# SwiGLU by seven products: 1024-column operations and two running sums in PSUM

## The chip, the cores and the metric

The kernel runs on one core of a Trainium2 chip. The metric is the device time of one execution in microseconds (us); a kernel's time is the median of its runs. The kernel computes in fp32 throughout, with every large matrix product split into three products of parts (see below).

## The reference

The model is a two-layer decoder on 512 tokens of width 1024. Each layer is half a SwiGLU, a mixer, and half a SwiGLU again, so there are four SwiGLUs, called ffn0 to ffn3 here. The change touches three of them; the mixers (`mlstm_mixer`, `nsa_shared_kv`, `nsa_mixer`) are left out.

```python
D_MODEL, SEQ, DEPTH, D_FF = 1024, 512, 2, 2816

def rmsnorm(x, g):
    xf = x.astype(jnp.float32)
    y = xf * lax.rsqrt(jnp.mean(xf * xf, axis=-1, keepdims=True) + EPS)
    return (y * g.astype(jnp.float32)).astype(x.dtype)

def swiglu(h, w_in, w_out):
    a, b = jnp.split(h @ w_in, 2, axis=-1)
    return (jax.nn.silu(a) * b) @ w_out

def reference(x, ...):
    h = x
    for layer in range(DEPTH):
        h = h + 0.5 * swiglu(rmsnorm(h, ffn_norm[layer, 0]), ffn_w_in[layer, 0], ffn_w_out[layer, 0])
        hn = rmsnorm(h, mix_norm[layer])
        ...
        h = h + 0.5 * swiglu(rmsnorm(h, ffn_norm[layer, 1]), ffn_w_in[layer, 1], ffn_w_out[layer, 1])
        ...
    return h
```

## The kernel before

Everything is held transposed: features lie on the 128 partitions and the 512 tokens along the columns, so the stream `h` is 8 tiles of 128 x 512. The stages run in the order ffn0, mlstm, ffn1, kv, ffn2, nsa, ffn3. The kernel is written in a tile language: a scheduler orders each engine's instructions ahead of time by its own estimate of durations, and each engine then runs its list strictly in that order, waiting on semaphores.

**Parts.** TensorE (PE) multiplies in a rounded fp32 format. So each operand is split (`split`, L232) into `hi`, its rounded value, made by ScalarE (ACT, L233), and `lo`, the rest, made by VectorE (DVE, L234). `mm3` (L226) then issues three matmuls into the same sum: hi by hi, hi by lo, lo by hi. Weights are split while they are loaded: `load_weight` (L135; L161 on ACT, L162 on DVE) for whole strips of 1024 columns, `load_forms` (L193) for the sums of quarters described next.

**Order of the weights.** A dry run first records in which order the weights are asked for (`plan`, `weight`). In the real run `weight` loads ahead in that order until `1 + self.ahead` are ready; `ahead` is 3 in the stages in question, and there are 4 buffers each for `whi` and `wlo`. So a split for the fourth weight from now waits until PE has finished with the oldest.

**One SwiGLU** (`ffn`, L364) has 22 blocks of 128 for the gate `a` and 22 for `b`, p = 0 to 21. They run in three chunks (`EVENS`: 8, 8 and 6 blocks), two blocks at a time. A pair of output blocks is computed either plainly (`strip`: 2 blocks x 8 k x 3 = 48 matmuls of 512 columns) or as a unit of seven products (`by_seven`, L447). In ffn0, ffn1 and ffn3 the blocks p = 0 and 1 (gate and `b`) and the gates of p = 2 and 3 are plain; there remain 9 gate units (`GATES`) and 10 `b` units, 19 per SwiGLU.

**A unit of seven products** halves the output rows (two blocks), the inner dimension (4 k each) and the tokens (256 each), and forms the product of these 2 x 2 matrices from seven products instead of eight: 7 x 4 k x 3 = 84 matmuls of 256 columns. The sums that it needs of the weight's quarters are made by `add_quarters` (L182, four DVE operations of 512 columns, L188 to L191), those of the tokens' quarters once per SwiGLU by `x_forms` (L411). Four DMAs of 256 KB fetch the quarters (`fetch`, L166), one unit ahead. The seven weight forms are split one at a time, 512 columns each. The products go to four PSUM banks X, Y, Z, V, and are put together by one ACT copy (L468) and five DVE operations, three of 256 columns (L473, L478, L488) and two of 512 (L476, L483).

**Gating.** `silu` (L389) multiplies the gate by the row scale `r` (L392, DVE) and takes Silu (L394, ACT), per block of 512 columns; `gate` (L397) multiplies by the `b` part (L401), in the last chunk also that part by `r` (L400, since `fold` is off there), and splits the result to `ghi`, `glo`.

**Output.** After each chunk, for each pair m of the 8 output blocks, `mm3` runs over that chunk's blocks (8, 8 or 6) into two PSUM banks; each block is then added to `h` (L589 and L590 where `fold`, L586 in the last chunk). For the pair m = 0 the order goes by k first, so that the freshest gated blocks are needed last. After the last chunk the next stage's `norm_in` (L265) reads `h`: it makes `xhi`, `xlo` and the sum of squares (L288, L300), which `rstd_columns` (L326) sums on PE.

ffn2 is computed from another stage's parts and its row of `LATER` chunks; it shares this code before the change and has a function of its own after it.

Of the kernel before, what the change touches and what calls it, by code (L numbers as in the profile page):

```python
# [30 lines left out]
SEVEN = (0, 1, 3)  # L31
# [67 lines left out]
class Net:  # L99
    def __init__(self, ctx, tc, a, order=None):  # L100
# [10 lines left out]
        self.raws, self.sums = {}, {}  # L111
# [23 lines left out]
    def load_weight(self):  # L135
# [4 lines left out]
        if name == "add":  # L140
            return self.add_quarters(*idx)
        if name == "form":
            self.ready.append(((name, idx), self.load_forms(*idx)))
            return
# [37 lines left out]
    def add_quarters(self, *at):  # L182

        q = self.raws[at]
        s = self.sums[at] = {j: self.fp.tile([P, 512], F32, name=f"s{j}", tag=f"s{j}", bufs=1) for j in (1, 2, 4)}
# [7 lines left out]
    def load_forms(self, i, p, group):  # L193

        q, s = self.raws[i, p], self.sums[i, p]
# [8 lines left out]
        return out  # L204

# [14 lines left out]
    def strip(self, w, k):  # L220
        return w[0][:, k, :], w[1][:, k, :]

    def mm(self, out, lhsT, rhs, start, stop):
        self.nc.tensor.matmul(out, lhsT, rhs, start=start, stop=stop)  # L224

    def mm3(self, out, l, r, start, stop):  # L226

        self.mm(out, l[0], r[0], start, False)
        self.mm(out, l[0], r[1], False, False)
        self.mm(out, l[1], r[0], False, stop)  # L230
# [6 lines left out]
    def setup(self):  # L237
        nc, a, c = self.nc, self.a, self.const
        self.h = [self.hp.tile([P, T], F32, name=f"h{b}") for b in range(KB)]
# [124 lines left out]
    def ffn(self, i, given=None):  # L364

        nc, tc = self.nc, self.tc
        seven, r = i in SEVEN, None
        self.qbufs = 2 if seven else 1
        self.ahead = 3 if seven else 2
        TT, STT = nc.vector.tensor_tensor, nc.vector.scalar_tensor_tensor  # L370
        N = T // 2
        with ExitStack() as ctx:
            pp = ctx.enter_context(tc.tile_pool(name=f"fps{i}", bufs=8 if seven else 6, space=PSUM, reuse_waits="tile"))
# [12 lines left out]
            x, ssq = (given, None) if given else self.norm_in(G_FFN + i * KB, True, i == 0)  # L386
            ps_mm = lambda: pp.tile([P, T], F32, name="pmm", tag="mm")

            def silu(pa):  # L389
                t = gp.tile([P, T], F32, name="ft", tag="ft", bufs=3 if seven else 2)  # L390
                if seven:
                    TT(t, pa, r, op=ALU.mult)  # L392
                    pa = t
                nc.scalar.activation(t, pa, AF.Silu)  # L394
                return t

            def gate(t, u):  # L397

                if seven and not fold:
                    TT(u, u, r, op=ALU.mult)  # L400
                TT(t, t, u, op=ALU.mult)  # L401
                bufs = 8 if seven or not k0 else 6
# [4 lines left out]

            def gate_plain(pa, pb):
                gate(silu(pa), pb)

            def x_forms(k):  # L411


                g1, g2 = (self.g[:, G_FFN + i * KB + b:G_FFN + i * KB + b + 1] for b in (k, k + 4))

                one, two = (gp.tile([P, 3 * N], F32, name="fw", tag="fw", bufs=3) for _ in range(2))
                h2, c = self.h[k + 4], [two[:, N * j:N * j + N] for j in range(3)]
                nc.scalar.activation(one[:, :T], self.h[k], AF.Copy, scale=g1)
                TT(one[:, T:], one[:, N:T], one[:, :N], op=ALU.subtract)
                STT(c[0], h2[:, N:], g2, one[:, T:], op0=ALU.mult, op1=ALU.subtract)  # L420
                STT(c[1], h2[:, N:], g2, one[:, N:T], op0=ALU.mult, op1=ALU.subtract)
                STT(c[2], h2[:, :N], g2, c[0], op0=ALU.mult, op1=ALU.subtract)
                hi = gp.tile([P, 4 * N], F32R, name="thi", tag="thi", bufs=4)
                lo = gp.tile([P, 4 * N], F32R, name="tlo", tag="tlo", bufs=4)
                self.split(one[:, T:], hi[:, :N], lo[:, :N])
                self.split(two, hi[:, N:], lo[:, N:])
                xt.append((hi, lo))
# [19 lines left out]
            def by_seven(p):  # L447
# [3 lines left out]
                W = gp.tile([P, 3, N], F32, name="fw", tag="fw", bufs=1 if i == 2 else 3)  # L451
# [42 lines left out]
            def plain(p):  # L494
                if seven and p == 1:
                    upcoming("fetch", None)
                w2 = [self.weight("ffn_in", i, p + j * FB) for j in range(2)]
                if seven and p == 1:
                    upcoming("add", None)
                ps = ps_mm(), ps_mm()  # L500
                order = [(k, j) for j in range(2) for k in range(KB)]
                if p == 0:
                    order.sort(key=lambda o: o[0] + 3.5 * o[1])
                for t, (k, j) in enumerate(order):
                    if seven and p == 1 and t == 3:
                        self.rstd_columns(ssq, ps_mm())
                    if seven and p == 1 and t >= 12:
                        x_forms(t - 12)
                    strip(ps[j], w2[j], k)
                    yield  # L510
                late.append(ps)

            xt, late = [], []


            if seven:
                units = [q for p in range(2, FB, 2) for q in ((p, FB + p) if p in GATES else (FB + p,))]
            else:
                units = [q for p in range(LATER[1][0], FB, 2) for q in (p, FB + p)][1:]
# [6 lines left out]
            for k0, k1 in EVENS if seven else LATER:  # L526
                gs, fold = [], seven and k1 < FB
# [914 lines left out]
```

## Time and profile before

| | |
|---|---|
| median of 3 runs | 1980.41 us (1978.17 to 1980.75) |
| profiled execution | 1979.33 us, its span 1976.4 us, so 2.9 us lie around the span |
| stages in question | ffn0 to 356.4 us; ffn1 from 575.5 to 930.0 us; ffn3 from 1626.4 us to the end |
| TensorE clock granted | 1.00 over the span |
| DMA | 98 GB/s in the mean |

Times in the trace count from the span's start. In a row of grouped instructions the shape stands as out<-in with partitions x elements, then the count, then busy time and the mean of one in ns, then the idle time of the engine just before them and who ended it. In the timeline a row has the start, the length and the instruction, with idle time before it in brackets. Instructions of one engine overlap in the records (an instruction starts before the row of the one before has ended), so what an instruction costs its engine is the distance between two starts. In the view of stretches each engine has its busy time in that stretch and, in brackets, how many of its instructions touch it.

### The profile page before, as it was taken

To read this page: it belongs to the slowest core of one execution; us is meant where nothing else is said; L and a number is where in the kernel's file an instruction comes from. 1 tells how busy PE (TensorE), PEld (TensorE's weight loads), DVE (VectorE), ACT (ScalarE), POOL (GpSimd) and SP (SyncE) were. 2 spreads that over 40 slices of the span, in tenths; PEclk is the share of its full clock that TensorE was granted. 3 is DMA by queue.
4 is the path that set the end of the run, shared out by engine and by line. 5 is a ranking of instruction groups with operands and counts; after the bars stand their busy time and mean duration, and the time that the engine had idled before them with its cause. 6 is when DMAs were issued, how large, how long until landed. Compare 5 with 4: busy or idle time off the path is not lost.

```text
span 1976.4 us, 31792 instructions
## 1 busy us (share of the span) xinstructions
PE 1958.3 (99%) x12042; PEld 1728.6 (87%) x12042; DVE 1611.1 (82%) x2960; ACT 1009.8 (51%) x1912; POOL 165.0 (8%) x217
## 2 busy tenths in 40 slices
PE   9999999999999999999999999999999999999999
PEld 7989999788879999898888989898777778999897
DVE  8969788757888879697687969686888888879795
ACT  6525345445655435254454535355889865435242
POOL 0000001012200000000110000001434420000000
PEclk9999999999999999999999999999999999999999
DMA  5333422323132323323443333323322132323322
GB/s 189 109 99 102 123 75 73 116 87 92 59 123 86 123 81 98 103 68 112 118 131 112 110 109 104 97 70 105 92 65 65 54 96 81 121 82 98 109 72 91
DMA packets 81816, 192.79 MB, mean 98 GB/s; under 512 B 9856, under 2 KB 10752, under 8 KB 81664
## 3 DMA queue, kind: packets, MB, share of 16 engines
q1 hardware_dynamic: 80272, 188.02, 31.2%
q8 instruction: 94, 1.54, 0.3%
q0 software_dynamic: 384, 1.05, 0.3%
q10 hardware_dynamic: 1008, 1.70, 0.2%
q14 instruction: 58, 0.48, 0.1%
HBM read 177.10 MB, written 2.10 MB: 91 GB/s over the span
## 4 chain that ended last, share of the span: by engine, by line
PE 83%; DVE 8%; ACT 4%; DMA 2%; issue 1%; SPq 0%; POOL 0%; DVEq 0%; ACTq 0%
PE pmm L224 76%; PE vps L224 2%; ACT pr L1181 1%; DVE wlo L162 1%; PE S L224 1%; PE po L224 1%; PE pt L1213 1%; PE paux L224 1%; DVE ptl L234 1%; DVE nx L1177 1%; DMA q<-in_ffn_in 1%; ACT pth L233 1%; PE pn L224 1%; DVE wlo L234 1%; ACT whi L161 0%
## 5 line engine op out<-in xcount | busy, mean ns | idle before, releaser
L224 PE MATMUL pmm<-xhi,whi 128*128 128x256 f32 (+1 forms) x1376 | 446.0, 324 | 0.9 <-ACT whi L161 0.4
L224 PE MATMUL pmm<-xhi,wlo 128*128 128x256 f32 (+1 forms) x1376 | 443.3, 322 | 0.6 <-DVE wlo L162 0.6
L224 PE MATMUL pmm<-xlo,whi 128*128 128x256 f32 (+1 forms) x1376 | 443.0, 322 | 0.5 <-DVE xlo L278 0.5
L161 ACT ACTIVATE whi<-wraw 128x512 fp32r<-128x512 f32 (+3 forms) x258 | 204.0, 810 | 313.9 <-PE pmm L224 183.2
L224 PE MATMUL pmm<-thi,wlo 128*128 128x256 f32 x1184 | 335.0, 283 | 1.0 <-DVE wlo L234 1.0
L224 PE MATMUL pmm<-tlo,whi 128*128 128x256 f32 x1184 | 335.3, 283 | 0.0
L224 PE MATMUL pmm<-thi,whi 128*128 128x256 f32 x1184 | 334.6, 283 | 0.1
L224 PEld LDWEIGHTS pmm<-xhi,wlo 128*128 128x128 f32 x1376 | 261.6, 190 | 20.5 <-DVE wlo L162 1.0
L224 PEld LDWEIGHTS pmm<-xlo,whi 128*128 128x128 f32 x1376 | 261.7, 190 | 19.1 <-DVE xlo L278 2.1
L224 PEld LDWEIGHTS pmm<-xhi,whi 128*128 128x128 f32 x1376 | 261.8, 190 | 18.8 <-issue 1.1
L162 DVE TENSOR_TENSOR wlo<-wraw,whi 128x512 fp32r<-128x512 f32 (+3 forms) x258 | 238.5, 936 | 45.1 <-ACT whi L161 42.7
L224 PE MATMUL pmm<-glo,whi 128*128 128x512 f32 x704 | 274.2, 390 | 0.1
L224 PE MATMUL pmm<-ghi,wlo 128*128 128x512 f32 x704 | 273.9, 389 | 0.0
L224 PE MATMUL pmm<-ghi,whi 128*128 128x512 f32 x704 | 272.6, 390 | 0.0
L233 ACT ACTIVATE whi<-s 128x512 fp32r<-128x512 f32 x222 | 139.5, 628 | 250.8 <-PE pmm L224 141.5
L224 PEld LDWEIGHTS pmm<-thi,wlo 128*128 128x128 f32 x1184 | 226.2, 191 | 1.2 <-DVE wlo L234 1.2
L224 PEld LDWEIGHTS pmm<-thi,whi 128*128 128x128 f32 x1184 | 226.8, 192 | 0.5 <-ACT fw L468 0.5
L224 PEld LDWEIGHTS pmm<-tlo,whi 128*128 128x128 f32 x1184 | 226.4, 191 | 0.0
L233 ACT ACTIVATE whi<-q 128x512 fp32r<-128x512 f32 x260 | 161.4, 623 | 117.8 <-PE pmm L224 103.0
L234 DVE TENSOR_TENSOR wlo<-q,whi 128x512 fp32r<-128x512 f32 x260 | 180.1, 693 | 16.2 <-ACT whi L233 16.0
L224 PEld LDWEIGHTS pmm<-glo,whi 128*128 128x128 f32 x704 | 132.2, 188 | 27.4 <-DVE glo L234 0.6
L224 PEld LDWEIGHTS pmm<-ghi,wlo 128*128 128x128 f32 x704 | 132.2, 188 | 27.4
(369 smaller groups left out, 3319.2 us busy)
## 6 DMA issues: line engine op xcount, KB each, us to landing
q<-in_ffn_in SPq DMA_DIRECT2D x260, 256.0 KB, 2.8
wraw<-in_ffn_out SPq DMA_DIRECT2D x48, 512.0 KB, 3.6
wraw<-in_ffn_out SPq DMA_DIRECT2D x48, 384.0 KB, 3.2
wraw<-in_ffn_in SPq DMA_DIRECT2D x27, 512.0 KB, 3.4
e<-in_ffn_in SPq DMA_DIRECT2D x36, 256.0 KB, 2.9
wraw<-in_m_qk SPq DMA_DIRECT2D x8, 512.0 KB, 3.3
wraw<-in_m_v SPq DMA_DIRECT2D x8, 512.0 KB, 3.3
wraw<-in_m_og SPq DMA_DIRECT2D x8, 512.0 KB, 3.3
```

What stands on the lines that cost most here:

```text
L161: nc.scalar.activation(hi[:p, c], raw[:p, c], AF.Copy)
L162: nc.vector.tensor_tensor(lo[:p, c], raw[:p, c], hi[:p, c].bitcast(F32), op=ALU.subtract)
L224: self.nc.tensor.matmul(out, lhsT, rhs, start=start, stop=stop)
L233: self.nc.scalar.activation(hi, src, AF.Copy)
L234: self.nc.vector.tensor_tensor(lo, src, hi.bitcast(F32), op=ALU.subtract)
L1177: nc.vector.tensor_reduce(nx[:, :m], S[:, :, :n], AX.X, ALU.max, negate=True)
L1181: nc.scalar.activation(s, S[:, i, :n], AF.Exp, bias=nx[:, i:i + 1], scale=cc, accum_out=z[:, i:i + 1])
L1213: nc.tensor.transpose(pt[:, col:col + P], pr[br][:, ROW[tb] + sb * P:ROW[tb] + sb * P + P], self.ident)
```

## The change

ffn0, ffn1 and ffn3 keep the seven products, the number and the width of all matmuls, the DMAs and the order in which the weights are asked for. What is different, with the names of the changed code:

- `quarters` fetches the four quarters into tiles laid side by side (`diag` holds a22 and a11, `low` a21, `right` a12 and one sum); `sums` makes the weight sums with one DVE operation of 1024 columns and two of 512.
- `wide_forms` splits the forms two at a time, 1024 columns per operation, the seventh alone.
- `by_seven` uses another set of seven products. Two of the PSUM sums run on: A takes three products and is copied out by ACT after the first and the second, the right half of B takes two and is copied out with its left half after the first. DVE then adds C and B (512 columns) and subtracts A (512 columns). In the diff the last argument of `product`, True, means that the product is added onto what the bank holds.
- `x_forms` makes four token forms into one tile of 1024 columns and splits them at once; before, the split was in two (256 and 768).
- Gating, Silu, the split of the gated blocks, and the output's additions to `h` take two blocks side by side, 1024 columns per operation; the output's pair is one PSUM tile of two banks. Only in the very last pair of ffn3 are the additions as before.
- PSUM is divided into 4 banks for single sums and 2 tiles of two banks; ffn2's code moves to `ffn_given` as it was.

```diff
+    def quarters(self, *at):
+        i, p = at
+        tile = lambda n, tag: self.fp.tile([P, n, 512], F32, name=tag, tag=tag, bufs=2)
+        diag, low, right = self.raws[at] = tile(2, "qd"), tile(1, "ql"), tile(2, "qr")
+        for t, j, a, b in (diag, 1, 0, 0), (diag, 0, 1, 1), (low, 0, 1, 0), (right, 0, 0, 1):
+            ap = self.a["ffn_in"][i, p + a, slice(None), slice(4 * b, 4 * b + 4)]
+            self.nc.sync.dma_start(t[:, j].rearrange("p (n m) -> p n m", m=P), ap)
+
+    def sums(self, *at):
+        diag, low, right = self.raws[at]
+        s = self.added[at] = self.fp.tile([P, 3, 512], F32, name="qs", tag="qs", bufs=1)
+        TT = self.nc.vector.tensor_tensor
+        TT(s[:, :2], diag, low.to_broadcast([P, 2, 512]), op=ALU.add)
+        TT(s[:, 2], s[:, 0], diag[:, 1], op=ALU.add)
+        TT(right[:, 1], s[:, 2], right[:, 0], op=ALU.add)
+
+    def wide_forms(self, i, p, group):
...
+        f = (diag, s[:, 0:3:2], right, s[:, 1:2])[group]
+        n = 1 if group == 3 else 2
...
+        self.split(f, v(hi), v(lo))
...
+            def by_seven(p):
+                A, CB = ps_mm()[:, :N], ps_two()
+                B, C = CB[:, 1], CB[:, 0, N:]
+                E = wide("ge" if p < FB else "ue")
+                e = E.rearrange("p j (c n) -> p (j c) n", n=N)
+                keep = lambda to, ps, scale=1.0: nc.scalar.activation(to, ps, AF.Copy, scale=scale)
...
+                upcoming("quarters", p)
+                a22, a11 = self.weight("forms", i, p, 0)
+                yield from product(A, a11, 0)
+                keep(e[:, 0], A)
+                yield from product(B[:, :N], a22, -4)
+                f1, f2 = self.weight("forms", i, p, 1)
+                yield from product(B[:, N:], f1, -1)
+                keep(E[:, 1], B, -1.0)
+                yield from product(A, f2, -2, True)
+                keep(e[:, 1], A)
+                a12, f4 = self.weight("forms", i, p, 2)
+                yield from product(C, a12, 2)
+                yield from product(B[:, N:], f4, 3, True)
+                TT(e[:, :2], e[:, :2], CB[:, :, N:], op=ALU.add)
+                f3 = self.weight("forms", i, p, 3)[0]
+                upcoming("sums", p)
+                yield from product(A, f3, -3, True)
+                TT(e[:, 2:], e[:, 2:], A[:, None, :].to_broadcast([P, 2, N]), op=ALU.subtract)
+                return E
+            def gate(t, u):
+                if not fold:
+                    TT(u, u, rows(), op=ALU.mult)
+                TT(t, t, u, op=ALU.mult)
+                finish(t)
+            def finish(t):
+                hi = gp.tile([P, 2, T], F32R, name="ghi", tag="ghi")
+                lo = gp.tile([P, 2, T], F32R, name="glo", tag="glo")
+                self.split(t, hi, lo)
+                gs.extend((hi[:, j], lo[:, j]) for j in range(2))
...
+                    po = ps_two()
...
+                    h = self.hh[m // 2]
+                    if fold:
+                        d = wide("fd")
+                        STT(d, po, 0.5, rows(), op0=ALU.mult, op1=ALU.mult)
+                        TT(h, h, d, op=ALU.add)
+                    elif i == 3 and m == KB - 2:
+                        for j, c in (0, slice(0, T)), (1, slice(0, N)), (1, slice(N, T)):
+                            STT(h[:, j, c], po[:, j, c], 0.5, h[:, j, c], op0=ALU.mult, op1=ALU.add)
+                    else:
+                        STT(h, po, 0.5, h, op0=ALU.mult, op1=ALU.add)
```

More of the change, by code (lines that the diff above doesn't have):

```diff
@@ new lines, in plain @@
+            def plain(p):
+                if p == 1:
+                    upcoming("quarters", None)
+                w2 = [self.weight("ffn_in", i, p + j * FB) for j in range(2)]
+                if p == 1:
+                    upcoming("sums", None)
+                ps = ps_two()
+                order = [(k, j) for j in range(2) for k in range(KB)]
+                if p == 0:
+                    order.sort(key=lambda o: o[0] + 3.5 * o[1])
+                for t, (k, j) in enumerate(order):
+                    if p == 1 and t == 3:
+                        self.rstd_columns(ssq, ps_mm())
+                    if p == 1 and t >= 12:
+                        x_forms(t - 12)
+                    strip(ps[:, j], w2[j], k)
+                    yield
+                late.append(ps)
@@ L374, in ffn, with ffn_given @@
+    def ffn_given(self, i, x):
+        nc, tc = self.nc, self.tc
+        self.qbufs = 1
+        self.ahead = 2
+        TT, STT = nc.vector.tensor_tensor, nc.vector.scalar_tensor_tensor
+        N = T // 2
+        with ExitStack() as ctx:
+            pp = ctx.enter_context(tc.tile_pool(name=f"fps{i}", bufs=6, space=PSUM, reuse_waits="tile"))
             inner, gp = ExitStack(), None
@@ L406, in gate @@
                 gs.append((hi, lo))
[L408 to L427, printed above, removed]
             def x_forms_late(k):
@@ L494, in plain @@
             def plain(p):
-                if seven and p == 1:
-                    upcoming("fetch", None)
                 w2 = [self.weight("ffn_in", i, p + j * FB) for j in range(2)]
-                if seven and p == 1:
-                    upcoming("add", None)
                 ps = ps_mm(), ps_mm()
[L501 to L511, printed above, removed]
+                for j in range(2):
+                    for k in range(KB):
+                        strip(ps[j], w2[j], k)
+                        yield
+                return ps
             xt, late = [], []
[L516 to L519, printed above, removed]
+            units = [q for p in range(LATER[1][0], FB, 2) for q in (p, FB + p)][1:]
             following = dict(zip([None] + units, units))
@@ L524, in upcoming @@
                     self.plan(what, i, following[p])
-            for k0, k1 in EVENS if seven else LATER:
-                gs, fold = [], seven and k1 < FB
-                if not seven and k0 == LATER[1][0]:
+            for k0, k1 in LATER:
+                gs = []
+                if k0 == LATER[1][0]:
                     brief.close()
@@ new lines, in ffn_given @@
+                for p in range(k0, k1, 2 if k0 else 1):
+                    if not k0:
+                        ps = yield from plain(p)
+                        gate(silu(ps[0]), ps[1])
+                        continue
+                    if p in units:
+                        ts = [silu(t) for t in (yield from by_seven(p))]
+                    else:
+                        ts = []
+                        for j in range(2):
+                            w = self.weight("ffn_in", i, p + j)
+                            if j:
+                                upcoming("fetch", None)
+                                upcoming("add", None)
+                            pa = ps_mm()
+                            for k in range(KB):
+                                strip(pa, w, k)
+                                yield
+                            ts.append(silu(pa))
+                    for t, u in zip(ts, (yield from by_seven(FB + p))):
+                        gate(t, u)
```

186 lines of the change are left out of this document (124 added, 62 removed).

## The prediction

> **What bounds the kernel now.** I read the page's totals and its chain first, then the stretches of the SwiGLUs one by one, then the distance between matmuls inside them.
>
> ```profile
> span 1976.4 us, 31792 instructions
> PE 1958.3 (99%) x12042; PEld 1728.6 (87%) x12042; DVE 1611.1 (82%) x2960; ACT 1009.8 (51%) x1912; POOL 165.0 (8%) x217
> PE 83%; DVE 8%; ACT 4%; DMA 2%; issue 1%; SPq 0%; POOL 0%; DVEq 0%; ACTq 0%
> ```
>
> PE is busy 99% of the span and holds 83% of the chain; DVE, which the change relieves, is the next engine. "Busy" alone proves little, since matmuls overlap in the records. So I take stretches with one kind of work in them: the units of seven products (first, third and last row), the output blocks between (second and fourth), and all of ffn1 behind its plain blocks.
>
> ```profile
> core 0: us, PE busy (x) PEld busy (x) DVE busy (x) ACT busy (x) POOL busy (x), PEclk, DMA share, GB/s
> 45.16:95.55 50.39, 50.39 (x421) 50.38 (x420) 50.22 (x89) 27.49 (x47) 0.00 (x0) 1.00 0.33 98
> 95.55:139.10 43.55, 43.55 (x194) 36.06 (x193) 28.16 (x40) 10.79 (x15) 0.00 (x0) 1.00 0.37 112
> 139.10:219.73 80.63, 80.63 (x673) 80.63 (x672) 77.90 (x138) 42.63 (x74) 0.00 (x0) 1.00 0.32 100
> 219.73:263.28 43.55, 43.55 (x194) 36.06 (x193) 27.42 (x39) 10.79 (x15) 0.00 (x0) 1.00 0.33 101
> ...
> 618.74:930.00 311.26, 311.26 (x2125) 290.66 (x2124) 261.52 (x433) 138.33 (x230) 4.88 (x4) 1.00 0.32 98
> 1754.83:1835.46 80.63, 80.63 (x674) 80.63 (x672) 77.92 (x138) 42.58 (x74) 0.00 (x0) 1.00 0.32 100
> ```
>
> The counts give the pace. Units: 420 matmuls in 50.39 us and 672 in 80.63 us are both 120.0 ns each, though DVE is at 99.7% in the one and 96.6% in the other; ffn3's stretch has the same 80.63 us to the hundredth. Output blocks: 192 matmuls in 43.55 us, 226.8 ns each, twice, with DVE at 65% and at 63%. (The counts of matmuls in the rows include one or two that cross an edge.) And the whole of ffn1 behind its plain blocks is 19 x 84 x 0.1200 + 22 x 8 x 3 x 0.2268 = 311.3 us at that pace, the row says 311.26: it loses nothing anywhere. A stretch that waited for DVE would not come out equal to one with another load. Single rows show the same pace, at the step from an output block to a unit:
>
> ```profile
> 138.65 0.39 PE L224 MATMUL pmm<-glo,whi 128*128 128x512 f32 x1
> 138.87 0.39 PE L224 MATMUL pmm<-ghi,wlo 128*128 128x512 f32 x1
> 139.10 0.28 PE L224 MATMUL pmm<-xhi,whi 128*128 128x256 f32 x1
> 139.22 0.28 PE L224 MATMUL pmm<-xlo,whi 128*128 128x256 f32 x1
> ```
>
> So a unit takes 84 x 0.120 = 10.08 us of PE, and 19 units in three SwiGLUs take 57 x 10.08 = 575 us, during which DVE is nearly full and nothing waits for it. That is the main reading: **the change lightens an engine that is full but not late.**
>
> **The change part by part.**
>
> *Matmuls.* 84 of 256 columns per unit before and after, the same plain blocks and output blocks. "Onto a standing sum" is no new form, which excludes a gain or a loss: in every product of before, 11 of 12 matmuls already add to what the bank holds, at the same 120 ns. Cost 0.
>
> *DVE.* Its cost is the distance between starts:
>
> ```profile
> 155.67 0.68 DVE L476 TENSOR_TENSOR fw<-fq,pmm 128x512 f32<-128x512 f32 x1
> 156.27 0.69 DVE L234 TENSOR_TENSOR wlo<-s,whi 128x512 fp32r<-128x512 f32 x1
> 156.87 0.41 DVE L478 TENSOR_TENSOR fu<-fw,pmm 128x256 f32<-128x256 f32 x1
> 157.20 0.69 DVE L234 TENSOR_TENSOR wlo<-q,whi 128x512 fp32r<-128x512 f32 x1
> ...
> 21.26 1.22 DVE L162 TENSOR_TENSOR wlo<-wraw,whi 128x1024 fp32r<-128x1024 f32 x1
> 22.40 0.69 DVE L190 TENSOR_TENSOR q<-q,q 128x512 f32<-128x512 f32 x1
> ```
>
> 512 columns 0.60 us (from PSUM too), 256 columns 0.33, 1024 columns 1.14. Before, a unit has 7 splits, 4 sums and 2 wide combinations (13 x 0.60) and 3 narrow ones (0.99): 8.79 us; a gate unit adds 2 x 0.60 for `r`, a `b` unit 4 x 0.60 for the product and `glo`. A pair of units: 9.99 + 11.19 = 21.18 us against 20.16 us of PE; the overhang is worked off in the output blocks. After: splits 3 x 1.14 + 0.60, sums 1.14 + 2 x 0.60, combinations 2 x 0.60, together 7.56 us; a gate unit + 1.14, a `b` unit + 2.28: a pair 18.54 us. DVE saves 2.64 us per pair, some 75 us over 57 units. On the path to the end this is worth 0, since PE keeps its 120 ns.
>
> *ACT.* It loses splits and gains three copies out of PSUM per unit.
>
> ```profile
> L233 ACT ACTIVATE whi<-q 128x512 fp32r<-128x512 f32 x29 | 18.0, 623 | 9.9 <-PE pmm L224 7.5 <-ACT whi L233 1.4 <-DVE fu L488 0.9
> L468 ACT ACTIVATE fw<-pmm 128x256 f32<-128x256 f32 x8 | 3.1, 384 | 7.1 <-PE pmm L224 7.1
> L161 ACT ACTIVATE whi<-wraw 128x1024 fp32r<-128x1024 f32 x2 | 2.1, 1062 | 1.5 <-PE pmm L224 1.5
> ```
>
> After: at most 3 x 1.06 + 0.62 for splits, 0.38 + 0.62 + 0.38 for copies, 1.06 for Silu or `ghi`: 6.2 of 10.08 us. It has room. (The 512-column copy out of PSUM is bounded by 0.38 and 1.06; I take the 0.62 of the same width.)
>
> *New waits.* Each running sum makes PE wait for an ACT copy: A goes on only when its copy is out, likewise B. Between the end of each such product and the next write lie two other products, 24 x 0.120 = 2.88 us. A copy takes 0.62 at most; with one 1024-column operation ahead of it in ACT's list it is done after 1.06 + 0.62 = 1.7 us. Covered, with 1.2 us to spare; queued behind a late copy would be PE itself, and everything for it. The Trainium skill (PSUM — Partial Sum Buffer, Bank collision) says that PE and ACT must not touch one bank at the same time and that software has to order them, which speaks against reading a sum in mid-run. By that alone each copy would cost its own 0.38 to 0.62 us; with two products between in other banks it gives 0, as my sum does, and no run so far shows such a copy in mid-run.
>
> *DMAs.* Four quarters of the same size per unit, asked for at the same place; SP and POOL issue nothing new. In another order: the first split now needs a11 and a22 at once. They are fetched one unit ahead (10 us). Cost 0.
>
> *The three ends of the units.* Here the wider operations can hurt, because an output needs its last blocks soon. In ffn3 before, output starts at 1939.48:
>
> ```profile
> 1939.48 0.40 PE L224 MATMUL pmm<-ghi,whi 128*128 128x512 f32 x1
> 1944.94 0.95 PE L224 MATMUL pmm<-ghi,whi 128*128 128x512 f32 x3
> 1946.01 0.51 PE L224 MATMUL pmm<-glo,whi 128*128 128x512 f32 x1
> ...
> 1940.27 0.68 DVE L400 TENSOR_TENSOR fw<-fw,r 128x512 f32<-128x512 f32 x1
> 1941.27 0.96 DVE L162 TENSOR_TENSOR wlo<-wraw,whi 128x768 fp32r<-128x768 f32 x1 [0.32 <-ACT whi L161]
> 1942.15 0.69 DVE L401 TENSOR_TENSOR ft<-ft,fw 128x512 f32<-128x512 f32 x1
> 1944.39 0.96 DVE L162 TENSOR_TENSOR wlo<-wraw,whi 128x768 fp32r<-128x768 f32 x1 [0.95 <-ACT whi L161]
> 1945.27 0.69 DVE L234 TENSOR_TENSOR glo<-ft,ghi 128x512 fp32r<-128x512 f32 x1
> ```
>
> Four older blocks cover 24 x 0.227 = 5.45 us, to 1944.93; from 1944.94 to 1946.01 three matmuls (0.68) take 1.07 us, so 0.39 are lost already. After: last product to about 1939.6, subtract A 0.7, times `r` 1.14, one weight split 0.88 (from 1941.27 to 1942.15), product 1.24, `ghi` 1.06, `glo` 1.24: 1945.9, where the first `glo` is wanted at 1945.2. The order of the matmuls is made ahead, as the three `ghi` in a row show, and the matmuls that need only `ghi` can bridge 0.7 us. Bounds per end: 0 and 2.0 (a second weight split, and the DMA late as here). I take 0.4 for ffn0 and ffn1 and 0 for ffn3, which has it already: + 0.8, between - 0.4 and + 5.6.
>
> *The two hand-overs,* ffn0 to mlstm and ffn1 to kv. The last pair is now added to `h` in one operation after both blocks.
>
> ```profile
> 356.63 0.69 DVE L586 SCALAR_TENSOR_TENSOR h<-pmm,h 128x512 f32<-128x512 f32 x1 [0.93 <-PE pmm L224]
> 359.19 0.69 DVE L288 TENSOR_TENSOR ssq<-ssq,sq 128x512 f32<-128x512 f32 x1
> 359.98 0.69 DVE L300 TENSOR_TENSOR ssq<-ssq,ssq 128x512 f32<-128x512 f32 x1
> ...
> 362.14 0.79 PE pnm L224 x8
> ```
>
> The sum of squares ends at 360.67 and PE takes it up at about 362.0 by the chain's order: 1.3 us to spare. After: + 0.54 (1.14 for 0.60) and the sixth block's `xlo` and square, which ran earlier, + 1.27: 1.8 us later, 0.5 too late at most. I take 0.25 each: + 0.5, between 0 and 1.0.
>
> *The start of ffn0.* PE's idle time there is what a lighter DVE could win at most:
>
> ```profile
> 0.00:38.00 38.00, 35.06 (x150) 27.31 (x150) 31.62 (x61) 25.53 (x40) 4.28 (x7) 1.00 0.69 238
> ```
>
> 38.00 - 35.06 = 2.94 us, most of it before x has landed and been split; `x_forms` changes little. I take 0, between - 2.9 and 0.
>
> **Sum.** 1979.33 + 0.8 + 0.5 = 1980.6 us, between 1979.33 - 0.4 - 2.9 = 1976.0 and 1979.33 + 5.6 + 1.0 = 1985.9, against the profiled execution's own time. The median of the runs, 1980.41, is 1.1 above that execution, and the lowest run 1.2 below it; I lean half way to the median: **1981.0 us**. Low 1976, high 1988 (1985.9 and two for that scatter). About 0.2%, 4 us, is what a measurement of this kernel can tell from no change.
>
> **The rivals.**
> 1. *PE waits for a copy in mid-sum* (slower). It decides when three 1024-column operations stand ahead of a copy in ACT's list: 3 x 1.06 + 0.38 = 3.6 us against 2.88, so 0.7 us lost. For: split, `ghi` and Silu are all of that width and the list is made ahead by estimates. Against: ACT would have 38% idle, and PE's present wait on L468's bank costs nothing. Once in every second unit: 28 x 0.7 = 20, 2001 us. Chance 0.08.
> 2. *The ends at their upper bound* (slower): + 6.6, 1986 us. For: ffn3's end already loses 0.39. Against: ffn0 and ffn1 lose nothing there now. Chance 0.10.
> 3. *PE has headroom* (faster). If the output blocks could run as fast as their weight loads, PEld's 36.06 of 43.55 us, each such stretch would give up to 7.5 us once DVE is lighter; with six of them and three shorter ones of 0.75 that size, 62 us: 1918 us. Against: the pace is 226.8 ns at any load of DVE. With it stands a start that wins over 4 us by another order of the first loads. Together 0.05. The Trainium skill (Perfetto Trace Analysis, Identifying the Most-Contended Engine) says to judge PE by its weight loads and not by busy matmuls, which for the whole span reads 87% and would put DVE's 82% close behind; the equal pace of the stretches goes against reading that gap as time to be won.
> 4. *The change does not do what it says*: a 1024-column operation from PSUM, or with a broadcast operand, costs as much as two. Then DVE stays at 97%, PE at 120 ns: 1980.4 us. Chance 0.05.
>
> The forecast has the remaining 0.72. Within 0.2%: 0.72 + 0.05 = 0.77; slower 0.08 + 0.10 = 0.18; faster 0.05. The range leaves out rivals 1 and 3, 0.13.
>
> **What would show it.** Right: units again at 84 x 0.120 us with DVE near 18.5 / 20.2 = 92% (and output stretches at 43.55 us), DVE's busy time down by some 75 us to about 1535, the span within 4 us. Step by step: PE's idle before the last chunk's `glo` (0 to 2 us), and before the matmuls that sum the squares in mlstm and kv (0 to 0.5). Wrong: distances over 120 ns inside units, ended by an ACT copy (rival 1); output stretches shorter than 43.5 us (rival 3); 1024-column distances near 1.2 us and DVE's load unchanged (rival 4).

## The result, and the profile after

The changed kernel takes 1997.72 us (median of 5 runs, 1997.05 to 2000.92), the kernel before beside it 1979.39: a ratio of 1.0097, with a 95% interval of 1.0083 to 1.0111. It is slower by 18.3 us, where a change of about 1 us had been forecast, and lies above the range of 1976 to 1988 us.

First the page of the changed kernel, its totals and the shares of its chain:

```profile
span 1999.1 us, 31202 instructions
PE 1971.3 (99%) x12042; PEld 1724.5 (86%) x12042; DVE 1539.4 (77%) x2394; ACT 1029.4 (51%) x1777; POOL 164.0 (8%) x217
PE 79%; DVE 11%; ACT 4%; DMA 2%; issue 2%; POOL 0%; SPq 0%; DVEq 0%; ACTq 0%; POOLq 0%
```

DVE is lighter by 1611.1 - 1539.4 = 71.7 us, as forecast (75), with the same 12042 matmuls. Still the span grew. This one execution is the slowest of the five; some three of its 22.7 us are its own. The view of stretches of the same execution says where much of the rest is: output blocks (first and third row), units of seven products between them, and the corresponding units of ffn3.

```profile
core 0: us, PE busy (x) PEld busy (x) DVE busy (x) ACT busy (x) POOL busy (x), PEclk, DMA share, GB/s
97.03:141.83 44.80, 44.80 (x194) 35.99 (x193) 20.70 (x18) 10.42 (x11) 0.00 (x0) 1.00 0.34 99
141.83:221.60 79.77, 79.77 (x673) 79.77 (x672) 74.31 (x82) 46.28 (x63) 0.00 (x0) 1.00 0.34 104
221.60:266.40 44.80, 44.80 (x195) 35.99 (x193) 20.70 (x18) 10.35 (x11) 0.00 (x0) 1.00 0.30 93
1776.04:1855.82 79.78, 79.78 (x673) 79.78 (x672) 74.31 (x82) 46.09 (x62) 0.00 (x0) 1.00 0.35 104
```

192 matmuls of an output stretch take 44.80 us, 233.3 ns each; before it was 43.55 and 226.8. No wait stands in the row, the clock is 1.00, and DVE's load has fallen to 46%. The units went the other way: 672 matmuls in 79.77 us, 118.7 ns for 120.0, with DVE at 93%. What excludes most explanations is ffn2, whose code the change doesn't touch. One of its output stretches (144 matmuls), in the kernel before and in the changed one:

```profile
1240.43:1273.08 32.65, 32.65 (x147) 27.04 (x145) 18.73 (x28) 8.66 (x14) 0.00 (x0) 1.00 0.34 97
```

```profile
1257.37:1290.97 33.60, 33.60 (x146) 27.00 (x145) 18.81 (x28) 8.67 (x14) 0.00 (x0) 1.00 0.35 96
```

The same 226.8 against 233.3 ns, at the same load of DVE and ACT. Four SwiGLUs have 528 such matmuls each: 2112 x 6.5 ns = 13.7 us. Taken apart by operand in the trace, the matmuls of the x-forms (the moving operands `thi`, `tlo`) went from 120.0 to 118.0 ns, 912 per SwiGLU, those of plain x halves from 120.0 to 119.7, 684 per SwiGLU: 3 x (1.8 + 0.2) = 6 us back. Net + 7.7 us.

The rest are waits. At the end of ffn0, PE and DVE in the view in order of time:

```profile
360.26 0.40 PE L258 MATMUL ptwo<-glo,whi 128*128 128x512 f32 x1
360.49 0.40 PE L258 MATMUL ptwo<-ghi,wlo 128*128 128x512 f32 x1
362.30 0.39 PE L258 MATMUL pg<-xhi,whi 128*40 128x512 f32 x1 [1.41 <-ACT hot L778]
```

```profile
360.93 1.22 DVE L585 SCALAR_TENSOR_TENSOR h<-ptwo,h 128x1024 f32<-128x1024 f32 x1 [2.48 <-PE ptwo L258]
362.07 1.28 DVE L166 TENSOR_TENSOR wlo<-wraw,whi 128x512 fp32r<-128x512 f32 x2
```

362.30 - 360.49 is 1.81 us where 0.23 is the rule. The bracket names ACT's `hot`, which ended last by the profile, but PE starts again 0.15 us after the 1024-column addition to `h` has ended (360.93 + 1.22 = 362.15). The end of ffn1 looks alike, 1.57 us at 939.1. And at the first unit of ffn0 PE waits for a PSUM tile that the gating of the plain blocks still reads (`ge`, L514), behind ACT's load of the table for Silu (45.15, 1.28 us):

```profile
46.33 0.28 PE L258 MATMUL pmm<-xhi,wlo 128*128 128x256 f32 x1
48.28 0.39 PE L258 MATMUL ptwo<-thi,whi 128*128 128x256 f32 x1 [1.68 <-DVE ge L514]
```

### The profile page after: what moved, and what is told of

Same layout as the page of the kernel before. It is cut to its first block, busy times and chain, and to the rows that moved or that the text cites. A ratio compares the mean times of both kernels' runs of the same rounds, so it can differ in the third digit from the quotient of the medians.

```text
span 1999.1 us, 31202 instructions
## 1 busy us (share of the span) xinstructions
PE 1971.3 (99%) x12042; PEld 1724.5 (86%) x12042; DVE 1539.4 (77%) x2394; ACT 1029.4 (51%) x1777; POOL 164.0 (8%) x217
## 4 chain that ended last, share of the span: by engine, by line
PE 79%; DVE 11%; ACT 4%; DMA 2%; issue 2%; POOL 0%; SPq 0%; DVEq 0%; ACTq 0%; POOLq 0%
PE pmm L258 37%; PE ptwo L258 33%; DVE wlo L268 2%; PE vps L258 2%; PE S L258 1%; PE po L258 1%; DVE wlo L166 1%; ACT pr L1348 1%; PE pt L1380 1%; PE paux L258 1%; DVE nx L1344 1%; DVE ptl L268 1%; PE pn L258 1%; DMA wraw<-in_ffn_out 1%; ACT pth L267 1%
## 5 line engine op out<-in xcount | busy, mean ns | idle before, releaser
L258 PE MATMUL pmm<-xhi,whi 128*128 128x512 f32 (+1 forms) x824 | 279.5, 339 | 1.4 <-DVE h L585 1.4
L258 PE MATMUL pmm<-xhi,wlo 128*128 128x512 f32 (+1 forms) x824 | 276.9, 336 | 0.0
L258 PE MATMUL pmm<-xlo,whi 128*128 128x512 f32 (+1 forms) x824 | 276.8, 336 | 0.0
L258 PE MATMUL ptwo<-ghi,whi 128*128 128x512 f32 x528 | 208.4, 396 | 0.6 <-ACT ghi L267 0.6
L258 PE MATMUL ptwo<-glo,whi 128*128 128x512 f32 x528 | 208.8, 395 | 0.0
L258 PE MATMUL ptwo<-ghi,wlo 128*128 128x512 f32 x528 | 208.5, 395 | 0.0
L258 PE MATMUL pmm<-tlo,whi 128*128 128x256 f32 x728 | 203.7, 280 | 0.0
L258 PE MATMUL ptwo<-xhi,whi 128*128 128x256 f32 (+1 forms) x552 | 167.5, 303 | 0.7 <-ACT whi L165 0.3
L258 PE MATMUL ptwo<-xhi,wlo 128*128 128x256 f32 (+1 forms) x552 | 166.6, 302 | 1.4 <-DVE wlo L166 1.4
L258 PE MATMUL ptwo<-xlo,whi 128*128 128x256 f32 (+1 forms) x552 | 166.8, 302 | 0.1
```

## The experiments

**Theory A** for the pace: the change allocates one small tile more, `less` (4 columns), in the pool `sp`, which lies ahead of the pools of all stages; all that is allocated behind it moves by 32 bytes per partition, in ffn2 too, and a matmul's pace depends on such addresses. **Rivals:** B, tiles of two PSUM banks and running sums have another pace; C, TensorE's pace goes with the load of VectorE. B and C have ffn2 against them from the start. The medians, of 4 to 11 runs each, beside the kernel before in the same batch (1978.29 to 1978.91 us):

| run | us | ratio to the kernel before, 95% interval |
|---|---|---|
| after_again | 1997.28 | 1.0103 (1.0088 to 1.0118) |
| less_at_home | 1991.07 | 1.0065 (1.0050 to 1.0080) |
| before_32_bytes_on | 1987.05 | 1.0049 (1.0034 to 1.0064) |
| last_pair_by_block | 1998.33 | 1.0107 (1.0090 to 1.0124) |
| last_pair_one_bank_each | 1995.12 | 1.0081 (1.0064 to 1.0098) |
| late_block_copied_out | 1995.86 | 1.0088 (1.0073 to 1.0103) |
| before_x_forms_32_on | 1983.96 | 1.0028 (1.0016 to 1.0040) |
| before_x_32_out_256_on | 1974.38 | 0.9977 (0.9965 to 0.9988) |
| after_mended | 1983.40 | 1.0017 (1.0009 to 1.0026) |
| before_x_192_out_256_on | 1973.04 | 0.9970 (0.9959 to 0.9981) |
| after_mended_x_192 | 1978.97 | 1.0002 (0.9993 to 1.0011) |

Three more kernels ran once each and are read for their paces alone: before_shifts_16_24_8_words (1983.70 us), before_shifts_32_40_48_words (1981.87) and before_all_32_bytes_on (1977.99).

**1. The changed kernel once more.**

> The changed kernel itself, once more. Every theory: 1997 to 1999 us. It separates what stands in every profile of it (output blocks at 233.3 ns a matmul in all four SwiGLUs, the x-form matmuls at 118.0 ns, 1.57 us lost at the end of ffn0 and of ffn1, 1.83 us at the first unit of ffn0) from what may be chance in the one profile seen so far (1.19 us at 584.21, 1.62 at 976.07, 1.52 at 1111.17, 1.74 at 1218.27): the former return, the latter need not.

1997.28 us. Both paces returned to the tenth of a nanosecond, the two hand-overs (1.58 and 1.57 us), and 1.11 us at the first unit; of the doubtful ones 1.62 in kv and 1.53 at the start of ffn2 returned, 1.74 inside ffn2 did not. At the end of mlstm a wait of 1.19 us is there in both profiles (below).

**2. The shift alone, and the change without it.**

```diff
# before_32_bytes_on, against the kernel before
+            if seven:
+                nc.vector.memset(self.sp.tile([P, 4], F32, name="less", tag="less"), 0.0)
# less_at_home, against the changed kernel
-            less = self.sp.tile([P, 4], F32, name="less", tag="less")
+            less = home[:, 4:8]
```

> The kernel before with nothing but a tile of four columns added to the pool `sp` in ffn0, ffn1 and ffn3, which moves what is allocated behind it by 32 bytes. Theory A: 512-column output blocks 233.3 ns (+13.7 us), x-form matmuls 118.0 ns (-6.3 us): about 1986.8 us. Rivals B and C: neither PSUM nor the engines' load changes, the paces stay at 226.8 and 120.0 ns, 1979.4 us.

> The changed kernel with the four columns of `less` in an unused part of the tile `home`, so that the pools behind `sp` lie where they lay before. Theory A (the addresses): the matmuls of the output blocks go back from 233.3 to 226.8 ns (2112 of them: -13.7 us) and those of the x-forms from 118.0 to 120.0 ns (+6.3 us in three SwiGLUs): about 1990.3 us. Rivals B (tiles of two PSUM banks, running sums) and C (a lighter VectorE changes TensorE's pace): nothing of the kind is touched, both paces stay, 1997.7 us.

1987.05 and 1991.07 us, both as theory A had it. The stretches of before_32_bytes_on, an output stretch and the units behind it:

```profile
94.99:139.79 44.80, 44.80 (x195) 35.99 (x194) 28.47 (x41) 10.82 (x15) 0.00 (x0) 1.00 0.37 110
139.79:219.57 79.78, 79.78 (x673) 79.78 (x672) 77.44 (x137) 42.87 (x74) 0.00 (x0) 1.00 0.31 99
```

and of less_at_home:

```profile
97.43:140.98 43.55, 43.55 (x194) 36.06 (x193) 20.70 (x18) 10.41 (x11) 0.00 (x0) 1.00 0.33 101
140.98:221.61 80.63, 80.63 (x673) 80.63 (x672) 74.31 (x82) 46.03 (x63) 0.00 (x0) 1.00 0.35 103
```

The kernel before, with one unused tile more, has the paces of the changed kernel (44.80 and 79.78); the changed kernel without it has those of before (43.55 and 80.63), with two-bank tiles, running sums and DVE at 92% of the units. B and C are out. The tile costs 8.8 us; the other parts of the change cost 12.8 (9.9 to 15.8), in the same batch of runs. The two make 21.6, where the whole change costs 19.0 there; the intervals, some 3 us to either side, leave room for that.

**3. Which addresses.** If each operand's own start counted, in steps of 128 bytes, one could keep the gain of the units and drop the loss of the output blocks.

```diff
# before_x_forms_32_on; before_x_32_out_256_on has 56 for 24, before_x_192_out_256_on 144 and 16
-            room(f"fg{i}")
+            room(f"fg{i}", 104 if seven else 96)
+            nc.vector.memset(gp.tile([P, 24], F32, name="pad", tag="pad", bufs=1)[:, :1], 0.0)
```

> The kernel before with its pools moved so that in ffn0, ffn1 and ffn3 the operands of the x-forms begin 32 bytes behind a multiple of 128, and those of the output blocks on one. Theory A (each operand's own address sets its matmuls' pace): x-form matmuls 118.0 ns, output blocks 226.8 ns, so only the gain of the shift is left: 1978.3 - 6.3 = about 1972 us. Rival A' (the shift of the whole pool matters, or of something else in it, such as the sums of the weights' quarters): the pace of the two goes together, and the time stays at 1978.3 or goes to 1987.

1983.96 us: neither. The x-forms took 118.0 ns, as expected, but the output blocks, 128 bytes on, 233.3. Other shifts, a different one in each SwiGLU:

```diff
# before_shifts_16_24_8_words; before_shifts_32_40_48_words has (32, 40, 0, 48)
-            room(f"fg{i}")
+            room(f"fg{i}", 96 + (16, 24, 0, 8)[i])
```

> The kernel before with the pools of ffn0, ffn1 and ffn3 moved by 64, 96 and 32 bytes (one look, for the paces only). Theory A1 (a start on a multiple of 64 bytes is as good as one on 128): ffn0 226.8 and 120.0 ns, ffn3 233.3 and 118.0, ffn1 as ffn3. Theory A2 (only multiples of 128 count): all three at 233.3 and 118.0. In both, ffn2, which is not moved, keeps 226.8 ns, and the time is between 1978 and 1985 us.

> The kernel before with the pools of ffn0, ffn1 and ffn3 moved by 128, 160 and 192 bytes (one look, for the paces). Theory A3: at 128 bytes the output blocks take 233.3 ns again, as the start of 0 modulo 256 did; 160 and 192 have not been seen, and are between 226.8 and 233.3. Rival A2 (only multiples of 128 count): 226.8 ns in ffn0, 233.3 in the other two. ffn2 is not moved: 226.8 ns.

Neither A1 nor A2: at 64 bytes the output blocks lay between (229.9), at 128 they were slow (232.4), and the x-forms had another pace at each shift. In the compiled program the weights `whi` and `wlo` begin at 128 modulo 256, as did all operands of before that had 226.8 ns. So two theories were left, the operand's own address modulo 256 (A3, A6), and its distance to the weights (A5), with A4 beside them.

> As before_x_forms_32_on, but with the operands of the output blocks 256 bytes on in place of 128 (the x-forms again 32). Theory A3 (a matmul's pace goes by the address of its moving operand modulo 256; the start that all fast ones share is 128 modulo 256): output blocks 226.8 ns, x-forms 118.0 ns: 1978.5 - 6.3 = about 1972 us. Rival A4 (the pace of the output blocks goes with the address of the x-forms or of other tiles of the units, not with their own): 233.3 ns again, about 1984 us.

> The kernel before with every SBUF tile but the x-forms of ffn2 moved by 32 bytes, the weights too (one look). Theory A5 (what counts is where the moving operand starts relative to the weights): 226.8 and 120.0 ns in ffn0, ffn1 and ffn3, about 1978.5 us; the x-forms of ffn2, which stay, change their pattern (118.7, 121.4, 120.0 ns for the three kinds of product) to that of a shift of 64 bytes (118.0, 118.3, 117.5). Rival A6 (the absolute address): 233.3 and 118.0 ns as with 32 bytes before, and the plain strips of x slow down from 227.2 to 233 ns as well: above 1987 us.

```diff
# before_all_32_bytes_on
+        nc.vector.memset(c.tile([P, 8], F32, name="pad"), 0.0)
         self.g = c.tile([P, G_N], F32, name="gains")
```

before_x_32_out_256_on took 1974.38 us, faster than the kernel before, and A4 is out: with the x-forms 32 bytes on and the output blocks moved by a whole 256, each has its better pace. Its stretches:

```profile
94.14:137.70 43.56, 43.56 (x195) 36.05 (x193) 28.65 (x41) 10.78 (x15) 0.00 (x0) 1.00 0.38 113
137.70:217.48 79.78, 79.78 (x673) 79.78 (x672) 77.44 (x137) 42.90 (x74) 0.00 (x0) 1.00 0.31 99
```

before_all_32_bytes_on, where operands and weights move together by 32 bytes, took 1977.99 us:

```profile
95.58:139.12 43.54, 43.54 (x194) 36.05 (x193) 28.06 (x40) 10.79 (x15) 0.00 (x0) 1.00 0.37 112
139.12:219.76 80.64, 80.64 (x674) 80.63 (x672) 77.91 (x138) 42.59 (x74) 0.00 (x0) 1.00 0.32 100
```

The paces are those of before, and the x-forms of ffn2, which stayed where they were, changed to the pattern of a shift of 64 (118.0, 118.1, 117.5 ns), as A5 said. What counts is **the distance between the moving operand and the weights, modulo 256 bytes**. That run is one execution, but its three SwiGLUs agree. All runs together, in ns per matmul (means over some 500 and 900 matmuls):

```
distance (bytes)                0      32     64     96     128    160    192
512 columns, output blocks    226.8  233.3  229.9  233.3  232.4  234.2  233.3
256 columns, x-forms          120.0  118.0  117.9  120.0  118.8  117.5  114.1
```

(At 128 another run had 233.3. 224 was not tried.)

**4. The hand-overs.** Theory A2 here: the next stage's first PSUM tile lies in the first bank of the last pair's tile of two, which one long addition reads.

```diff
# last_pair_by_block
-                    elif i == 3 and m == KB - 2:
+                    elif m == KB - 2:
# last_pair_one_bank_each: the last pair, where not folded
+                    po = [ps_mm() for _ in range(2)] if last else ps_two()
+                        if last and k == n - 1:
+                                STT(hj, po[j][:, c], 0.5, hj, op0=ALU.mult, op1=ALU.add)
```

> The changed kernel with the last pair of output blocks of ffn0 and ffn1 added to h in three pieces, block by block, as ffn3 has it already. Theory A2 (the first PSUM tile of the next stage lies in the bank that the 1024-column addition still reads): the bank is read out some 1.2 us earlier, up to 1.57 us come back at each of the two ends: 1994.6 to 1996 us. Rival (what is late there is the sum of squares or the load of the activation table, behind the whole addition): 1997.7 us or a little more, from one more instruction each.

> The changed kernel with the last two output blocks of ffn0, ffn1 and ffn3 each in a PSUM tile of one bank, each added to h as soon as it is done (the last of ffn3 in two halves, as before). Theory A2 (hand-overs and tail are late by the tile of two banks: its first half can't be read before its second is written, and the next stage begins in its first bank): the 1.57 us at 360.3 and at 939.0 and 1.0 us of the tail go, 4.1 us: 1993.2 us. Rival (the next stage waits for the sum of squares or for its first operand, whatever the bank): the waits come back under another name, 1996 to 1997.3 us.

By block alone nothing came: 1998.33 us, and the waits are 1.71 us. The row of DVE in last_pair_by_block tells why:

```profile
360.85 1.35 DVE L583 SCALAR_TENSOR_TENSOR h<-ptwo,h 128x512 f32<-128x512 f32 x3 [2.48 <-PE ptwo L258]
```

All three pieces start after the pair's last matmul (360.42): in this program the first half of a tile is not read while its second half is being written. That disposes of a sentence on the change, too: the additions of ffn3's last pair are "as before" in their pieces only. Before, the first block was added at 1968.91, four us ahead of the last two pieces (1972.99); in after_again all three pieces stand at 1990.72, and the time from the last matmul's start to the span's end is 1 us longer. With a tile for each block, PE's rows at the end of ffn0 in last_pair_one_bank_each:

```profile
360.92 0.39 PE L258 MATMUL pmm<-ghi,wlo 128*128 128x512 f32 x1
361.14 0.40 PE L258 MATMUL pg<-xhi,whi 128*40 128x512 f32 x1
```

No wait, though the last addition begins only at 361.34: it was the bank, not the sum of squares. The compiled programs say the same: the next stage's first tile lies in bank 0 in each of them, and ffn0's last pair in banks 0 and 6 before (bank 0 has the block that is added early), 0 and 1 after, 6 and 4 here. Both hand-overs and the 1 us of the tail are gone from the trace, 1.57 + 1.57 + 1.0 = 4.1 us. The median fell by less, 2.2 us against after_again, with overlapping intervals, and the profiled span by 1.0 us: this execution has 0.7 us more at the first unit of ffn0, 1.0 more in kv and 1.3 more in nsa, places that the edit doesn't touch. So 4.1 us is the size of the waits that went, and the medians alone don't show it.

**5. The first unit of ffn0.**

```diff
# late_block_copied_out
+                nc.scalar.activation(u[:, 0], late[0][:, 1], AF.Copy)
```

> The changed kernel with one more ScalarE copy in each of ffn0, ffn1 and ffn3, which takes the second half of the first late tile out of PSUM before the activation table is loaded, so that the first unit's tile is free earlier. Theory: the 1.1 to 1.8 us lost in ffn0 before the first unit's first matmul into that tile go: 1995.5 to 1996.2 us. Rival (what is late there is the x-forms' split or the weights): the wait stays, 1997.3 to 1998 us.

1995.86 us lies in the theory's range, but by luck. In the profile the next stage begins at 364.07, 2.0 us later than in after_again, so ffn0 has gained nothing; what made the median smaller was not found, and its interval overlaps that of after_again. The wait at the first matmul is gone and another stands 4 us later: in ACT's list, some way behind the table load, a copy of a running sum is queued behind three operations of 1024 columns (48.97 to 51.92). PE's rows in late_block_copied_out:

```profile
50.44 0.28 PE L258 MATMUL pmm<-thi,wlo 128*128 128x256 f32 x1
52.45 0.39 PE L258 MATMUL ptwo<-xhi,whi 128*128 128x256 f32 x1 [1.73 <-ACT ue L439]
```

What is late there is ACT; whether moving the table load would mend it was not tried.

**6. The change at equal addresses.** after_mended has `less` in `home`, the shifts of before_x_32_out_256_on and the single tiles of last_pair_one_bank_each.

```diff
# after_mended, beside the edit of last_pair_one_bank_each; after_mended_x_192 has 144 and 16
+            home = gp.tile([P, 104], F32, name="home", tag="home", bufs=1)
+                nc.vector.memset(gp.tile([P, 56], F32, name="pad", tag="pad", bufs=1)[:, :1], 0.0)
-            less = self.sp.tile([P, 4], F32, name="less", tag="less")
+            less = home[:, 4:8]
```

> The changed kernel with `less` in `home`, the x-forms 32 bytes on, the output blocks 256 bytes on, and the last pair in tiles of one bank. Theory: of the 18.9 us that the change costs, 13.7 go by the output blocks' address and 2 to 4 by the last pair; the x-forms keep their 118.0 ns: 1979.5 to 1981.5 us, no different from before, and slower than the kernel before with the same shifts (1972 us). Rival A4: the output blocks stay at 233.3 ns, 1993 to 1995 us.

1983.40 us, 2 to 4 us above what was expected, and 9.0 above its pair, before_x_32_out_256_on. By stages, from the two profiles (11.6 us apart): ffn0 + 3.6, mlstm + 1.8, ffn1 + 0.5, kv + 3.0, ffn2 + 2.4, nsa + 0.6, ffn3 - 0.2. ffn0 is the first unit (1.73), the end of the units (0.49) and the start. mlstm is its end, where the first unit's sums are made ahead; DVE there in the changed kernel:

```profile
583.20 1.78 DVE L313 SCALAR_TENSOR_TENSOR xlo<-h,gains,xhi 128x512 fp32r<-128x512 f32 x1
584.90 0.68 DVE L1024 TENSOR_TENSOR h<-pmm,h 128x512 f32<-128x512 f32 x1
585.50 0.68 DVE L226 TENSOR_TENSOR qr<-qs,qr 128x512 f32<-128x512 f32 x1
```

PE waits 1.03 us, to 585.63, for the addition at 584.90. The `xlo` ahead of it takes 1.78 us, where it took 0.74 before: DVE's other order has put it beside a sum of squares on POOL (582.96, 1.47 us). In the profiles of before and after every `xlo` of more than 1 us, 5 and 8 of them, runs beside such an addition, and none away from one takes more than 0.76; that POOL is the cause was not tested by a run. kv and ffn2 hold waits of 1.5 us that other executions have too, and behind some of them a stretch at a lower granted clock (last section). The scatter of this kernel, 1979.17 to 1985.42 us, goes with that clock: the runs with a mean of 1.000 took 1979.2 to 1981.9 us, those with 0.997 took 1985.3 and 1985.4. Between the fastest runs of the pair the distance is 5.5 us.

**7. Does the lighter DVE pay when PE is faster?** At a distance of 192 bytes the x-forms' matmuls take 114.1 ns.

> As before_x_32_out_256_on, with the x-forms 192 bytes on in ffn0, ffn1 and ffn3, where their matmuls took 114.1 ns in the one look, and VectorE was late: stalls of 5.2 us in that ffn3 against 1.3 in before_x_32_out_256_on. Theory A7 (a TensorE that is faster in the units runs into VectorE, which is busy for nearly all of them): the 3 x 912 x 3.9 ns = 10.7 us that the matmuls save come back as waits for about 3 x 3.9 us: 1974 us, the same as with 32 bytes. Rival A8 (the stalls of that ffn3 were the slow output blocks' or chance): 1974.4 - 10.7 = 1963.7 us.

> As after_mended, with the x-forms 192 bytes on. Theory A7: VectorE is busy for 90 to 93% of the units here, so that the whole 10.7 us come: 1983.4 - 10.7 = 1972.7 us, and the change, slower by 9.0 us where the x-forms take 118.0 ns, is about even with its pair. Rival A8: both get as much, and the distance to before_x_192_out_256_on stays at 9 us. Rival A9 (something else of the changed units has no room, ScalarE or the splits of the weights): 1980 to 1983 us, with waits in the units.

1973.04 and 1978.97 us. The kernel before gained 1.3 of the 10.7 us, the changed one 4.4. A unit stretch of before_x_192_out_256_on, the output stretch behind it, and PE's waits in the latter:

```profile
138.41:216.50 78.09, 78.09 (x674) 78.09 (x672) 75.93 (x135) 42.34 (x74) 0.00 (x0) 1.00 0.31 99
216.50:262.46 45.96, 44.39 (x195) 35.88 (x193) 29.27 (x43) 10.85 (x15) 0.00 (x0) 1.00 0.34 104
```

```profile
PE pmm L224 <- DVE glo L234: 0.8, 1, 0.8
PE pmm L224 <- DVE wlo L162: 0.5, 1, 0.5
```

The units run at 116.2 ns, and their overhang on DVE is paid in the output blocks, as waits for DVE's splits: that is A7. The same stretches of after_mended_x_192:

```profile
139.92:219.35 79.43, 79.23 (x673) 78.63 (x672) 74.28 (x82) 46.45 (x62) 0.00 (x0) 1.00 0.35 104
219.35:262.89 43.54, 43.54 (x195) 36.04 (x193) 20.70 (x18) 10.42 (x11) 0.00 (x0) 1.00 0.32 96
```

No wait in the output blocks, but 1.34 us more in eight units: that is A9, by the copies of the running sums, `ue`. One of them, on PE and on ACT:

```profile
174.78 0.28 PE L258 MATMUL pmm<-thi,wlo 128*128 128x256 f32 x1
175.12 0.39 PE L258 MATMUL ptwo<-xhi,whi 128*128 128x256 f32 x1
175.34 0.28 PE L258 MATMUL ptwo<-xlo,whi 128*128 128x256 f32 x1
```

```profile
173.52 1.06 ACT L537 ACTIVATE ge<-ge 128x1024 f32<-128x1024 f32 x1
174.49 0.58 ACT L440 ACTIVATE ue<-ptwo 128x512 f32<-128x512 f32 x1
```

The copy starts behind a Silu of 1.06 us, and PE goes on only when it has ended (175.07). This step and the one behind it take 0.34 and 0.22 us for 0.11 and 0.12; three such places in the stretch, at 174.78, 194.71 and 214.65, make 1.0 of the 1.34 us, and the same step in the other units most of the rest. The view of waits lists only larger ones, which stand elsewhere in the span (total, times, longest):

```profile
PE ptwo L258 <- ACT ue L440: 2.0, 5, 0.5
```

The matmul that waits there is the first of C, which lies in the first bank of the tile of two (`CB[:, 0, N:]`), while the copy reads B, the second (`CB[:, 1]`). B itself is written again only one product later. So here too the tile is waited for as a whole; whether C in a tile of its own would take the wait away was not tried.

So DVE's relief is worth some 3 us at this pace, a third of what the change costs at equal addresses, and that is rough, since the runs of the changed kernels scatter over 6 us. Nothing tried makes the changed kernel faster than before; the version that beats both is the kernel before with its operands shifted, before_x_192_out_256_on, 0.9970 (0.9959 to 0.9981).

## Why the prediction was wrong

**The step that failed is *Matmuls*, "Cost 0".** It looked at number, width and form, and at a pace that was the same at any load of DVE, and took 226.8 and 120.0 ns for constants of PE. They held between the loads of DVE, and less_at_home gives them back to the hundredth; but they belonged to a placement of the operands. The change added a tile in a pool that all stages share, and the sum had no term for where things lie: + 13.7 us in the output blocks, - 6 in the units, net 7.7 by the paces and 8.8 by the time of before_32_bytes_on. Added to the forecast of 1981.0 us this alone would give 1988.7. Rival 3 had asked whether these paces can move, and tied that to DVE's load alone.

*The two hand-overs* failed in cause and size: 0.25 each, at most 0.5, through the sum of squares; measured 1.57 each, through the PSUM bank of the last pair, which last_pair_one_bank_each showed. The step followed who needs the sums of `h`, and not who needs the tile that they are made from.

*The three ends of the units* were near: 0.37 and 0.58 us in ffn0 and ffn1 where 0.4 was taken, none new in ffn3 (0.99 in ffn0 of after_again, 1.18 in ffn1 of less_at_home). But the kernel's own end, 1.0 us, was in no term.

*The start of ffn0*: its first 38 us have the idle time of before (3.01 us for 2.94), as forecast; in after_again it is 3.29. The first unit behind it, 1.1 to 1.8 us, and mlstm's end, 1.8 us in after_again, were in no term either.

*DVE* and *ACT* were right: DVE came down by 71.7 us to 93% of the units, worth nothing at the pace of that time. *New waits* had the right size, and its room wrong: behind the first unit of ffn0 no wait inside the changed units is over 0.24 us, but between the end of B's first part and the next write to its tile lies one product, 1.44 us, and not two, 2.88, because C lies in that tile. By the step's own 1.7 us for a copy behind one operation, that is not covered. So Rival 1's mechanism exists with fewer than three operations ahead of the copy: it shows once PE is faster (0.2 us and more at a time), and with three ahead in late_block_copied_out (1.73 us). The Trainium skill (PSUM — Partial Sum Buffer, PSUM bank collisions raise a hardware error), weighed there for a copy in mid-run, asks for semaphores that keep two engines out of one bank. It would have been of more use at the hand-overs, where the trace agrees with it: the next stage's first matmul waits 1.57 us for DVE's read of that bank.

Of the 18.7 us between the profiles of before and after_again, the addresses hold 7.7, the hand-overs and the tail 4.1, mlstm's end 1.8, the ends of the units 1.5 (0.99 and 0.55), the first unit 1.1, together 16.2; the other 2.5 lie in ffn0 (0.6), ffn1 (0.7) and kv (1.2), and were not pursued.

## What to carry to other kernels

Before a change is costed, see what it allocates ahead of other tiles: a pace per matmul read off a trace holds for the placement of its operands, and a stretch of untouched code that changes its pace is the sign that it moved. A tile of two banks was one thing here to whoever waited for it: nothing of it was free, readable or writable before all of it was. And an engine's relief is worth what the next engine leaves of it, which can be measured by making that next engine faster.

## What the runs showed of the hardware

The pace of a stream of matmuls goes with the distance of the moving operand to the weights modulo 256 bytes, by 3% at 512 columns and 5% at 256, and not the same way for both. The Trainium skill (TensorE: Matmul & The Clock Gate, Step-by-step: what each phase is for) says that the weights' loads and the moving operand have SBUF read ports of their own, so that loading takes no read bandwidth from the running matmul; these runs (114.1 to 120.0 ns by the distance alone) speak against full independence; where the two meet was not settled.

A short wait of PE can cost more than itself. In after_mended, four stretches around a wait of 1.53 us at the start of ffn2:

```profile
1098.00:1102.00 4.00, 3.75 (x23) 3.15 (x21) 3.05 (x7) 1.96 (x4) 0.00 (x0) 1.00 0.00 0
1102.00:1104.00 2.00, 0.58 (x3) 0.37 (x3) 2.00 (x5) 2.00 (x6) 0.00 (x0) 1.00 0.10 18
1104.00:1108.00 4.00, 4.00 (x21) 4.00 (x22) 4.00 (x7) 2.47 (x6) 0.00 (x0) 0.57 0.53 155
1108.00:1112.00 4.00, 4.00 (x35) 4.00 (x34) 4.00 (x9) 1.30 (x3) 0.00 (x0) 1.00 0.54 170
```

Behind the wait the granted clock is 0.57 in the mean of 4 us, and 21 matmuls run where 35 do after them. Inside that stretch it is 0.50 for 3.41 us:

```profile
1104.33:1107.74 3.41, 3.41 (x18) 3.41 (x18) 3.41 (x7) 1.88 (x5) 0.00 (x0) 0.50 0.46 144
```

The same wait passed without this in after_again. Of some forty waits of 1.3 to 2.0 us in the sixteen profiles, six were followed within 2.1 us by such a stretch (after, late_block_copied_out, after_mended twice, after_mended_x_192, before_x_192_out_256_on). Six more such stretches begin in nsa, between 1389 and 1414 us, behind a group of waits. The profile of before has none; what decides was not found. The Trainium skill (TensorE: Matmul & The Clock Gate, HAM oscillation — how this bites in real kernels) asks for no idle gaps of PE over about 3.4 us; here half of that was enough at times.
